# A ring of SBUF places in another order, P tiles as slices of one tile, and 21 instead of 19 weights asked for ahead, in a kernel that streams its weights

## The chip, the cores and the metric

The kernel runs on one core of one Trainium2 chip. The metric is the device time of one execution in microseconds (us). An execution is profiled once for the trace; the time is taken from several further runs.

## What is computed

Everything is float32, with 256 tokens of 1024 columns. A first block has two layers, each a token mixer with two kinds of attention and then a layer of experts; a second block has a mixer of a gated scan and a long convolution, and then a mixture of 32 experts. From the reference, cut:

```python
def first_block(x, ...):
    h = x
    for l in range(2):
        h = h + hybrid_mixer(rmsnorm(h, norm_mix[l]), w_in[l], ...)
        h = h + expert_choice_ffn(rmsnorm(h, norm_ffn[l]), w_router[l],
                                  w_expert_gate[l], w_expert_up[l], w_expert_down[l])
    return rmsnorm(h, norm_final)

def expert_choice_ffn(h, w_router, w_gate, w_up, w_down):   # 16 experts, 32 tokens each
    aff = softmax(h @ w_router)
    gate, idx = top_k(swapaxes(aff, 1, 2), 32)
    xe = h[bidx, idx]
    a, u = einsum('becd,edf->becf', xe, w_gate), einsum('becd,edf->becf', xe, w_up)
    ye = einsum('becf,efd->becd', silu(a) * u, w_down)
    return zeros_like(h).at[bidx, idx].add(gate[..., None] * ye)
...
# second block: adaLN (shift, scale and gate from silu(c) @ ada_w), a token mixer,
# then hier_moe: 4 groups of 8 experts, the best group and its best 2 experts per token
        hid = silu(einsum('td,edf->tef', t, w_gate[gi])) * einsum('td,edf->tef', t, w_up[gi]) \
            * combine[:, gi, :, None]
        out = out + einsum('tef,efd->td', hid, w_down[gi])
```

## The kernel before

The weights are some 746 MB and are read once. Nearly each is cut into pieces of 128 partitions x 2048 float32, 1 MB, and each piece is fetched by one DMA (`fetch`, issued at L58) into a tile `w`. All fetches go through SP's queue in the order of the program, each held behind the one before it (`issue_after`): a fetch whose place isn't free holds up all that are behind it.

The places are named by tags. `W` has 9 places of 1 MB and holds weights alone. `T` has 12 of the same size, which weights share with the large activations (the names in `WHOLE`: `x`, `hTa`, `qa`, `hn` and others). Small tags hold tiles of 2 KB per partition: `P` and `PT` four each (`NP`), `wh` and `wl` three each. Within a tag the places go round: the n-th tile of a tag with k places takes the place of the (n-k)-th and waits until that one's last reader is done. `K.use(places)` sets a string of tags that `chunk` goes through, one letter for each weight: for "WT" every other weight asks for a W place and every other for a T place.

The program in order of time (us of the trace): the first mixer; expert stage of layer 0 (`experts`), whose later part is interleaved with the mixer of layer 1 (`ahead`); expert stage of layer 1, interleaved with the preparation of the second block's filters and context states (`prep`); the token mixer (`token_mixer`); routing, and the MoE (`moe`, `moe_round`, `moe_quad`) to the end. Ahead of each expert stage a prefetch asks for the first weights while the mixer and the routing still work: `ROOM`, 19 tags, in the two layers, and `ROOM2`, 16 tags, in the MoE. Behind it the ring is "WT" (layer 0), `FEW` (layer 1) or "WWTWT" (MoE). In the layers a weight of `w_eg` is used by 4 instructions in L810, which the trace shows as 8 rows, two for each float32 matmul, and gives its place back after them; a MoE weight of `w2eg` is used likewise in L1485, where two weights are used in turns, a quarter of their 16 rows each. Gather matmuls (L889, L1458) lie in between while the gathered tokens of a group of experts are built. The last matmuls of the stages are L863 (`w_ed`) and L1524 (`w2ed`).

In the mixers a weight of a projection is split on the way: ScalarE rounds 512 of its columns to `wh` (L101), VectorE or POOL takes the remainder to `wl` (L102), and each product is three matmuls (L121 to L123), hTa with wh, hTb with wh, hTa with wl. A weight is thus 48 matmuls.

Attention works in rounds on tiles of tag P: mask and maximum (VectorE, L414), exponential (ScalarE, L417), scaling (VectorE, L506), transposes (PE, L434). Tag P also holds `gb` (`ada_gate`, L632 and below: a 256 KB row of biases that is fetched behind the four `ada` weights of a gate), `gs` (the gate and up products of an expert) and `yt` (a product of the MoE). `ada_gate` runs twice: in the token mixer, ahead of its weights (w2z, w2q, ...), where L174 (the squares of a norm, `sq`) was the last to use the place that `gb` takes; and behind the routing, ahead of the prefetch of the MoE, where POOL's `h` of L1317 was the last to read it.

At the start of the token mixer eight tiles `ht` (L1050, ScalarE, tag PT) are cast to `hTa` (L1051) and their remainder to `hTb` (L1052), both on VectorE.

Of the kernel before, what the change touches and what calls it, by code (L numbers as in the profile page):

```python
# [2 lines left out]

# [1 line left out]

# [4 lines left out]
F = mybir.dt.float32  # L10
# [7 lines left out]
T, D = 256, 1024  # L18
# [4 lines left out]
PW = 2048  # L23
# [9 lines left out]
class Core:  # L33
    def __init__(self, ctx, tc, A):
        self.tc, self.nc, self.A = tc, tc.nc, A
        self.const = ctx.enter_context(tc.tile_pool(name="const", bufs=1))
        self.sb = ctx.enter_context(tc.tile_pool(name="sb", bufs=1))
        self.ps = ctx.enter_context(tc.tile_pool(name="ps", bufs=1, space=PSUM))
        self.flip = self.nsplit = self.nchunk = 0

        self.share = 4
        self.after = nullcontext
        self.idle, self.pre, self.sent = (), [], None
        self.use("W")

    def load(self, name, shape, dt=F):
        t = self.const.tile(shape, dt, name=name)
        self.fetch(t, name)
        return t

    def use(self, places):

        self.ring = cycle(places)

    def fetch(self, out, src):

# [3 lines left out]
    def chunk(self, src, parts=1):  # L60

        tag = next(self.ring)
        t = self.sb.tile([128, PW], F, name="w", tag=tag, bufs=PLACES[tag])
        n = src.shape[1] // parts
        for i in range(parts):
            self.fetch(t[:, i * n:(i + 1) * n], src[:, i * n:(i + 1) * n])
        return t

    def next_chunk(self, src, parts=1):
        return self.pre.pop(0) if self.pre else self.chunk(src, parts)  # L70
# [3 lines left out]

    def t(self, shape, name, bufs=1, tag=None, dt=F):
        tag = tag or name
        if tag in WHOLE:
            tag, bufs = "T", PLACES["T"]
        return self.sb.tile(shape, dt, name=name, tag=tag, bufs=bufs)
# [122 lines left out]
class Quarters:  # L202

    shape = (128, PW)
# [9 lines left out]
class Ahead:  # L214
# [14 lines left out]
    def dest(self, j):  # L229

        for t, n, o in ((self.qk[0], 4, 0), (self.qk[1], 2, 0), (self.raw, 4, 0), (self.qk[1], 1, 4), (self.Ga, 4, 0), (self.Gb, 4, 0)):
            if j < n:
                return t[:, o + 2 * j:o + 2 * j + 2, :]
            j -= n
# [57 lines left out]
HEAD = ((1, 3), (0, 3))  # L292

WHOLE = {"x", "hTa", "hTb", "qa", "qb", "qc", "V", "G", "hgw", "hn", "ob"}
ROOM2 = "TWWTTTTWWTTTWWWW"
ROOM, FEW = "TWWWWTTTTTTWWTTTWWW", "WWWWTWWWWWT"
PLACES = {"W": 9, "T": 12}
NP = 4
SMALL = {"P": NP, "PT": NP, "wh": 3, "wl": 3, "oa": 2}
BANKS = {"mm": 2, "sc": 2, "tp": 2, "acc": 2}  # L300
# [21 lines left out]

def mixer(K, h, l, ada, first=None, ahead=None):
    nc, A = K.nc, K.A
    if ahead:
        x = ahead.x
        ahead.turned(3)
    else:
        w_in = iter(A["w_in"])

        K.idle = range(K.nsplit + HEAD[l][0], K.nsplit + HEAD[l][1])
        x = K.pair("hT")
        K.transposed(h, lambda kb, p: K.split_to(x[0][:, kb, :], x[1][:, kb, :], p, K.gmix[:, l, kb:kb + 1]),
                     banks=("tp", "sc"))
# [286 lines left out]
def ada_gate(K, g):  # L621

    nc = K.nc
    p = K.bank("acc")
    for c in range(4):
        w = K.chunk(K.A["ada"][2, 4 * g + c])
        with K.after():
            for j in range(4):
                nc.tensor.matmul(p[32 * j:32 * j + 32, :], lhsT=K.cs32[:, 2 * c + j // 2, :],
                                 rhs=w[:, j * 512:(j + 1) * 512], start=(c == 0), stop=(c == 3),  # L630
                                 tile_position=(0, 32 * j))
    gb = K.t([128, 512], "gb", NP, tag="P")  # L632
    K.fetch(gb, K.A["gtb"][g])
    K.ms = K.t([128, 512], "ms", tag="wr")
    nc.vector.tensor_add(K.ms, p, gb)
# [81 lines left out]
def experts(K, h, l, mix, ada, prep, ahead=None):  # L717
    nc, A = K.nc, K.A
# [3 lines left out]
    next(rt)  # L722
    for _ in mix:
        next(rt)
    q = K.logits
    rs = K.rstd(h, dve=False, tag="oa")
    lg = K.t([128, 2, NE], "lg")
# [64 lines left out]

    K.use(ROOM)
    ws = [K.chunk(A["w_eg"][l, i // KD, i % KD]) for i in range(len(ROOM))]
    K.use("WT" if ahead else FEW)
    hid, Ge = [], []
    gw = K.t([128, 4], "gw4")
    for e in range(NE):
        if e == 2:
            for _ in gather(1):  # L800
                pass
        oh, xT = ohs[e // 8], xTs[e // 8]
        gu = K.bank("mm")
        for k in range(KD):
            if e >= 4 and k % 3 == 2:
                next(prep, None)
            next(ga, None)
            w = ws.pop(0) if ws else K.chunk(A["w_eg"][l, e, k])
            for j in range(4):
                nc.tensor.matmul(gu[32 * j:32 * j + 32, :], lhsT=xT[:, k, (e % 8) * CAP:(e % 8 + 1) * CAP],  # L810
                                 rhs=w[:, j * 512:(j + 1) * 512], start=(k == 0), stop=(k == KD - 1),
                                 tile_position=(0, 32 * j))
        if e == 0:
            for _ in ada:
                pass
        if e % 8 == 0:
            hid.append(K.t([128, 8, 4, 64], "hid", tag=own[e // 8]))
        gs = K.t([128, 512], "gs", NP, tag="P")
        K.copy(gs, gu)
        p = K.bank("tp")  # L820
        for fb in range(4):
            nc.tensor.transpose(p[:, fb * 128:(fb + 1) * 128], gs[:, fb * 128:(fb + 1) * 128], K.ident)  # L822
        pv = p.rearrange("p (a b) -> p a b", a=4)
        sg = K.t([128, 512], "sg", NP, tag="PT")[:, :256].rearrange("p (a b) -> p a b", a=4)
        nc.scalar.activation(sg, pv[:, :, 0:64], AF.Silu)  # L825
        nc.vector.tensor_mul(hid[-1][:, e % 8], pv[:, :, 64:128], sg)  # L826
        if e % 8 == 7:

            p, q = K.bank("tp"), K.bank("acc")
            for y in range(2):  # L830
                for tt in range(2):
                    o4 = oh[:, tt, 4 * y:4 * y + 4].rearrange("p a b -> p (a b)")
                    nc.tensor.transpose(p[:, (2 * y + tt) * 128:(2 * y + tt + 1) * 128], o4, K.ident)
                for tt in range(2):
                    o4 = oh[:, tt, 4 * y:4 * y + 4].rearrange("p a b -> p (a b)")
                    nc.tensor.matmul(q[:, 4 * y:4 * y + 4], lhsT=o4, rhs=aff[:, tt, e - 7 + 4 * y:e - 3 + 4 * y],
                                     start=(tt == 0), stop=(tt == 1))
                for x in range(4):
                    nc.vector.tensor_copy(gw[32 * x:32 * x + 32, e // 8 * 2 + y:e // 8 * 2 + y + 1],
                                          q[32 * x:32 * x + 32, 4 * y + x:4 * y + x + 1])  # L840
            Ge.append(K.t([128, 2, T], "Ge4", 2, tag="oa", dt=FR))
            K.copy(Ge[-1].rearrange("p a b -> p (a b)"), p)
# [188 lines left out]

def token_mixer(K, h):
    nc, A, tc = K.nc, K.A, K.tc

    sc = K.t([128, 2, D], "sincos", tag="V")
    K.fetch(sc, "sincos")
# [9 lines left out]
    x = K.pair("hT")  # L1046
# [282 lines left out]
def moe(K, h, mix):  # L1329
    nc, A, tc = K.nc, K.A, K.tc  # L1330
# [11 lines left out]
    next(rt)  # L1342
    for _ in mix:
        next(rt)
    q = K.logits
    rs = K.rstd(h, dve=False, tag="oa")
    K.after = lambda: tc.issue_after(K.routed.ins)
# [79 lines left out]

    K.use(ROOM2)
    K.pre = [K.chunk(A["w2eg"][2 * i + x, c]) for i in range(2) for c in range(4) for x in range(2)]
    K.use("WWTWT")  # L1430

    def gate(*args):
        spread_gate(*args)
# [36 lines left out]
def moe_quad(K, h, xT, oh, cmb, e, i, gate):  # L1470

    nc, A = K.nc, K.A
    hid = []
    work = K.t([128, 2, 1024], "work", tag="G")
    for pr in range(2):
        gu = K.bank("mm")
        for c in range(4):
            ws = [K.next_chunk(A["w2eg"][e + 2 * pr + x, c]) for x in range(2)]
            for kk in range(2):
                k = 2 * c + kk  # L1480
                for x in range(2):
                    for j in range(2):
                        o = 64 * x + 32 * j
                        y = (i + 2 * pr + x) * CAP2
# [3 lines left out]
        gs = work[:, pr, 0:512]  # L1488
# [27 lines left out]
    for hf in range(2):  # L1516
        sl = slice(hf * 512, (hf + 1) * 512)
        dn = K.bank("acc")
        end = e + 4 + hf == NE2 + 1

        wd = [K.next_chunk(A["w2ed"][e + x, hf], 4 if end and x == 3 else 1) for x in range(4)]
        for c in range(4):
            for x in range(4):
                nc.tensor.matmul(dn[32 * x:32 * x + 32, :], lhsT=hid[x][:, c, :], rhs=wd[x][:, c * 512:(c + 1) * 512],  # L1524
                                 start=(c == 0), stop=(c == 3), tile_position=(0, 32 * x))
        y = K.t([128, 512], "yt", NP, tag="P")
        nc.vector.scalar_tensor_tensor(y, dn, gw, K.gt[:, 1, sl], op0=OP.mult, op1=OP.mult)
        hi, lo = yd[:, 0, sl], yd[:, 1, sl]
        K.split_to(hi, lo, y)
        for tt in range(2):  # L1530
            p = K.bank("sc")
            for n, part_ in enumerate((hi, lo)):
                nc.tensor.matmul(p, lhsT=Ge[:, tt * 128:(tt + 1) * 128], rhs=part_, start=(n == 0), stop=(n == 1))
            hs = h[:, tt, sl]
            nc.vector.tensor_add(hs, p, hs)
# [214 lines left out]
```

## Time and profile before

| | |
|---|---|
| median of 3 runs | 2229.97 us (2227.25 to 2230.5) |
| the profiled execution, its own time | 2231.4 us |
| its span in the trace | 2229.6 us |
| PE busy | 1803.5 us, 81% |
| DVE, ACT, POOL busy | 761.1, 600.3, 222.2 us |
| read from HBM | 745.74 MB, 335 GB/s over the span |
| mean granted TensorE clock | 0.915 |

Times of the trace count from the span's start. PE, ACT, DVE, POOL and SP are TensorE, ScalarE, VectorE, GpSimd and SyncE. The busy share of PE is a mean over stages: in the expert stages the DMA engines run at up to 422 GB/s and PE waits, in the mixers PE is full and the DMA engines are not. SP only issues DMAs; its waits are those of the queue of weights.

### The profile page before, as it was taken

How to read it: one execution, taken by the hardware profiler on the slowest of the kernel's cores; microseconds unless marked ns; L12 is line 12 of the kernel's file. 1: busy time of each engine (PE TensorE's matmuls, PEld its weight loads, DVE VectorE, ACT ScalarE, POOL GpSimd, SP SyncE). 2: the span in 40 equal slices, each digit the busy share in tenths (PEclk: the TensorE clock that was granted, in tenths of full speed). 3: DMA queues.
4: the chain of work that ended last, by engine and by line, in shares of the span. 5: the costliest groups of instructions: out<-in, count | busy, mean ns of one | idle time of the engine just before them, and what ended most of it. 6: DMA issues, size and time to landing. Idle time of an engine off the chain costs nothing.

```text
span 2229.6 us, 30070 instructions
## 1 busy us (share of the span) xinstructions
PE 1803.5 (81%) x12172; PEld 1017.9 (46%) x12172; DVE 761.1 (34%) x1696; ACT 600.3 (27%) x1191; POOL 222.2 (10%) x183
## 2 busy tenths in 40 slices
PE   8999996666699998987788666789999867676765
PEld 8888631110277776841234123368888412121211
DVE  5666510000045588532111111157557311111112
ACT  4666410000033357620125100055245200000000
POOL 2111200000011122300000000033134000000000
PEclk9999997777799999997799778889999999999998
DMA  8445779999999953569999999984223999999996
GB/s 342 149 146 207 313 311 420 422 421 421 421 418 419 414 210 151 216 264 399 420 420 420 421 419 420 418 337 156 76 70 149 418 420 421 420 421 421 421 421 284
DMA packets 108442, 748.83 MB, mean 336 GB/s; under 512 B 14120, under 2 KB 14537, under 8 KB 18697
## 3 DMA queue, kind: packets, MB, share of 16 engines
q1 hardware_dynamic: 107752, 745.79, 82.3%
q8 instruction: 98, 1.61, 0.3%
q10 hardware_dynamic: 544, 1.05, 0.1%
q14 instruction: 48, 0.39, 0.1%
HBM read 745.74 MB, written 1.05 MB: 335 GB/s over the span
## 4 chain that ended last, share of the span: by engine, by line
PE 40%; DMA 29%; issue 22%; DVE 6%; ACT 2%; POOL 0%; POOLq 0%; SPq 0%; ACTq 0%; DVEq 0%
DMA w<-in_w_eg 18%; DMA w<-in_w_ed 9%; PE mm L121 7%; PE mm L122 6%; PE mm L123 6%; PE acc L863 4%; PE mm L810 3%; PE sc L889 2%; DVE wl L102 1%; PE acc L518 1%; DMA w<-in_w2z 1%; PE acc L949 1%; PE acc L1228 1%; DMA cx<-in_ctx 1%; PE sc L122 1%
## 5 line engine op out<-in xcount | busy, mean ns | idle before, releaser
L810 PE MATMUL mm<-w,xT 128*32 128x512 f32 x2048 | 327.8, 743 | 116.6 <-DMA w<-in_w_eg 116.2
L101 ACT ACTIVATE wh<-w 128x512 fp32r<-128x512 f32 x384 | 239.9, 630 | 290.5 <-PE mm L122 218.0
L121 PE MATMUL mm<-hTa,wh 128*128 128x256 f32 x960 | 281.0, 294 | 5.6 <-DVE Ga L245 1.7
L123 PE MATMUL mm<-hTa,wl 128*128 128x256 f32 x960 | 274.2, 288 | 1.9 <-DVE wl L102 1.6
L122 PE MATMUL mm<-hTb,wh 128*128 128x256 f32 x960 | 272.5, 285 | 2.2 <-DVE hTb L113 1.6
L102 DVE TENSOR_TENSOR wl<-w,wh 128x512 fp32r<-128x512 f32 x286 | 220.1, 775 | 108.9 <-ACT wh L101 106.1
L1485 PE MATMUL mm<-w,xT 128*32 128x512 f32 x1024 | 176.9, 613 | 71.9 <-DMA w<-in_w2eg 71.4
L863 PE MATMUL acc<-w,hid 128*32 128x256 f32 x2048 | 184.7, 449 | 62.3 <-DMA w<-in_w_ed 62.3
L102 POOL TENSOR_TENSOR wl<-w,wh 128x512 fp32r<-128x512 f32 x98 | 129.0, 1317 | 901.9 <-ACT wh L101 803.9
L810 PEld LDWEIGHTS mm<-w,xT 128*32 128x32 f32 x2048 | 51.3, 120 | 329.6 <-DMA w<-in_w_eg 271.6
L121 PEld LDWEIGHTS mm<-hTa,wh 128*128 128x128 f32 x960 | 181.8, 190 | 28.4 <-issue 15.7
L123 PEld LDWEIGHTS mm<-hTa,wl 128*128 128x128 f32 x960 | 181.0, 190 | 10.6 <-issue 3.4
L122 PEld LDWEIGHTS mm<-hTb,wh 128*128 128x128 f32 x960 | 182.0, 190 | 6.2 <-issue 2.4
L863 PEld LDWEIGHTS acc<-w,hid 128*32 128x32 f32 x2048 | 80.5, 128 | 148.6 <-DMA w<-in_w_ed 83.1
L1524 PE MATMUL acc<-w,work 128*32 128x512 f32 x512 | 94.9, 640 | 32.9 <-DMA w<-in_w2ed 32.9
L1485 PEld LDWEIGHTS mm<-w,xT 128*32 128x32 f32 x1024 | 34.2, 110 | 189.1 <-DMA w<-in_w2eg 140.8
L178 POOL TENSOR_TENSOR rs<-rs,mhalf 128x2 f32<-128x2 f32 x9 | 6.8, 751 | 1008.4 <-DVE rs L177 1008.4
L826 DVE TENSOR_TENSOR hid<-tp,sg 128x256 f32<-128x256 f32 x32 | 13.6, 425 | 216.8 <-ACT sg L825 216.8
L113 DVE SCALAR_TENSOR_TENSOR yd<-acc,gw,yd 128x256 fp32r<-128x256 f32 x32 | 15.5, 483 | 181.2 <-ACT yd L112 181.2
L112 ACT ACTIVATE yd<-acc,gw 128x256 fp32r<-128x256 f32 x32 | 15.2, 475 | 220.0 <-PE acc L863 220.0
L91 DVE COPY gs<-mm 128x512 f32<-128x512 f32 x16 | 11.1, 692 | 181.5 <-PE mm L810 181.5
L825 ACT ACTIVATE sg<-tp 128x256 f32<-128x256 f32 x32 | 12.3, 384 | 218.3 <-PE tp L822 218.3
(468 smaller groups left out, 2471.8 us busy)
## 6 DMA issues: line engine op xcount, KB each, us to landing
w<-in_w_eg SPq DMA_DIRECT2D x256, 1024.0 KB, 19.8
w<-in_w_ed SPq DMA_DIRECT2D x128, 1024.0 KB, 18.5
w<-in_w2eg SPq DMA_DIRECT2D x128, 1024.0 KB, 19.8
w<-in_w2ed SPq DMA_DIRECT2D x63, 1024.0 KB, 19.8
w<-in_ada SPq DMA_DIRECT2D x24, 1024.0 KB, 11.7
w<-in_w_in SPq DMA_DIRECT2D x22, 1024.0 KB, 7.2
w<-in_wk SPq DMA_DIRECT2D x20, 1024.0 KB, 17.7
w<-in_w_b SPq DMA_DIRECT2D x8, 1024.0 KB, 6.0
```

The costliest lines, as they stand in the source:

```text
L101: self.hi = nc.scalar.activation(hi, src, AF.Copy)
L102: (nc.gpsimd if n in self.idle or n % self.share == self.share - 1 else nc.vector).tensor_tensor(lo, src, hi.bitcast(F), OP.subtract)
L121: mm(out, lhsT=l[0], rhs=r[0], start=start, stop=False)
L122: mm(out, lhsT=l[0], rhs=r[1], start=False, stop=False)
L123: mm(out, lhsT=l[1], rhs=r[0], start=False, stop=stop)
L518: nc.tensor.matmul(po[half * 64:half * 64 + 64, :T], lhsT=V[:, kt, c:c + 64], rhs=PTs[half][:, kt * 256:(kt + 1) * 256], start=(kt == 0), ...
L810: nc.tensor.matmul(gu[32 * j:32 * j + 32, :], lhsT=xT[:, k, (e % 8) * CAP:(e % 8 + 1) * CAP], rhs=w[:, j * 512:(j + 1) * 512], start=(k == ...
L863: nc.tensor.matmul(dn[32 * x:32 * x + 32, :T], lhsT=hid[e // 8][:, e % 8, f, hh * 32:hh * 32 + 32], rhs=ws[x][:, fb * T:(fb + 1) * T], sta ...
L889: nc.tensor.matmul(p[:, :T], lhsT=hn[:, tt, kb * 128:(kb + 1) * 128], rhs=oh[:, tt].rearrange("p a b -> p (a b)"), start=(tt == 0), stop=( ...
L949: nc.tensor.matmul(p[:, :T], lhsT=w[:, o:o + 128], rhs=cT[:, k, :], start=(k == 0), stop=(k == KD - 1))
L1485: nc.tensor.matmul(gu[o:o + 32, :], lhsT=xT[:, k, y:y + CAP2], rhs=ws[x][:, (2 * kk + j) * 512:(2 * kk + j + 1) * 512], start=(k == 0), st ...
L1524: nc.tensor.matmul(dn[32 * x:32 * x + 32, :], lhsT=hid[x][:, c, :], rhs=wd[x][:, c * 512:(c + 1) * 512], start=(c == 0), stop=(c == 3), ti ...
```

## The change

The prefetches become longer: 21 weights in the layers and 18 in the MoE (16 of `w2eg` and the first two of `w2ed`). One of them, the letter "Q", lies in four quarters of 256 KB in three `wh` places and one `wl` place; one more lies in a 13th T place. Behind the prefetch the ring repeats the tags of the prefetch in its own order (`AGAIN`, `AGAIN2`), without the first two T (which become activations) and without Q; in layer 1 `AGAIN` runs once and then `FEW`. The 13th T place comes from tag P: a P tile is now one of four slices of 512 columns of one T tile (`K.held`), which is taken anew where `K.held` is set to None. `gb`, `gs` and `yt` move from tag P to tag PT.

```diff
-    def use(self, places):
-        self.ring = cycle(places)
+    def use(self, places, first=""):
+        self.ring = chain(first, cycle(places))
...
     def chunk(self, src, parts=1):
         tag = next(self.ring)
+        if tag == "Q":
+            return self.quarters(src, ("wh", "wh", "wh", "wl"))
...
+    def quarters(self, src, tags):
+        ts = []
+        for i, tag in enumerate(tags):
+            ts.append(self.sb.tile([128, 512], F, name="w4", tag=tag, bufs=SMALL[tag]))
+            self.fetch(ts[-1], src[:, i * 512:(i + 1) * 512])
+        return Quarters(ts)
...
         tag = tag or name
+        if tag == "P":
+            if self.held is None:
+                self.held = self.sb.tile([128, PW], F, name="P4", tag="T", bufs=PLACES["T"]), cycle(range(0, PW, 512))
+            o = next(self.held[1])
+            return self.held[0][:, o:o + shape[1]]
...
-ROOM2 = "TWWTTTTWWTTTWWWW"
-ROOM, FEW = "TWWWWTTTTTTWWTTTWWW", "WWWWTWWWWWT"
-PLACES = {"W": 9, "T": 12}
+AGAIN, AGAIN2 = "WWWWTTTTTTWWTTTWWW", "WWTTTTWWTTTWWWW"
+ROOM2 = "TTWWTTTTWWTTQTWWWW"
+ROOM, FEW = "TTWWWWTTTTTTWWTTQTWWW", "WWWWTWWWWWT"
+PLACES = {"W": 9, "T": 13}
...
-    gb = K.t([128, 512], "gb", NP, tag="P")
+    gb = K.t([128, 512], "gb", NP, tag="PT")
...
-    K.use("WT" if ahead else FEW)
+    K.use(AGAIN if ahead else FEW, AGAIN)
...
-        gs = K.t([128, 512], "gs", NP, tag="P")
+        gs = K.t([128, 512], "gs", NP, tag="PT")
...
+    K.pre += [K.chunk(A["w2ed"][x, 0]) for x in range(len(ROOM2) - 16)]
-    K.use("WWTWT")
+    K.use(AGAIN2)
...
-        y = K.t([128, 512], "yt", NP, tag="P")
+        y = K.t([128, 512], "yt", NP, tag="PT")
```

`K.held = None` is added at the start of `mixer` and `token_mixer` and in both routings. Line numbers behind the first changes are some 16 to 23 higher in the changed kernel; L58 stays.

Two places in the order of the instructions. On SP, the `gb` of the token mixer and the weights behind it; the brackets give the engines whose signals an instruction waits for (DMAHW is the queue itself). Before:

```order
509 L58 DMA w<-in_ada 128x2048 [waits DMAHW6_49,PE_49]
510 L58 DMA gb<-in_gtb 128x512 [waits DMAHW7_49,Activation_49]
511 L58 DMA w<-in_w2z 128x2048 [waits DMAHW0_49,PE_49]
512 L58 DMA w<-in_w2z 128x2048 [waits DMAHW1_49,PE_49]
515 L58 DMA w<-in_w2q 128x2048 [waits DMAHW4_49,PE_49]
```

and of the change:

```order
515 L58 DMA w<-in_ada 128x2048 [waits DMAHW4_49,PE_49]
516 L58 DMA gb<-in_gtb 128x512 [waits DMAHW5_49,DVE_49,Activation_49]
517 L58 DMA w<-in_w2z 128x2048 [waits DMAHW6_49,PE_49]
518 L58 DMA w<-in_w2z 128x2048 [waits DMAHW7_49,PE_49]
521 L58 DMA w<-in_w2q 128x2048 [waits DMAHW2_49,PE_49]
```

`gb` stands where it stood, and now waits for VectorE too, for the subtraction that is the last to read the fifth `ht`. On VectorE, in the same place of the program, the casts and subtractions of the eight `ht`, `ms` (which adds `gb`) and the first `wl` of w2z. Before:

```order
955 L635 TENSOR_TENSOR ms<-acc,gb 128x512
956 L1051 CAST hTa<-ht 128x256
957 L1052 TENSOR_TENSOR hTb<-ht,hTa 128x256
958 L1051 CAST hTa<-ht 128x256
959 L102 TENSOR_TENSOR wl<-w,wh 128x512
960 L1052 TENSOR_TENSOR hTb<-ht,hTa 128x256
961 L102 TENSOR_TENSOR wl<-w,wh 128x512
```

and of the change:

```order
966 L1073 TENSOR_TENSOR hTb<-ht,hTa 128x256 x2
967 L1072 CAST hTa<-ht 128x256
968 L1073 TENSOR_TENSOR hTb<-ht,hTa 128x256
969 L1072 CAST hTa<-ht 128x256
970 L1073 TENSOR_TENSOR hTb<-ht,hTa 128x256 x2
971 L654 TENSOR_TENSOR ms<-acc,gb 128x512
972 L118 TENSOR_TENSOR wl<-w,wh 128x512 x15
```

`ms` and all of `wl` have moved behind the eight subtractions. And on SP, the second `gb`, behind the routing, with the prefetch of the MoE behind it. Before:

```order
550 L58 DMA w<-in_ada 128x2048 [waits DMAHW7_49,DVE_49,Pool_49]
551 L58 DMA gb<-in_gtb 128x512 [waits DMAHW0_49,Activation_49,Pool_49]
552 L58 DMA w<-in_w2eg 128x2048 [waits DMAHW1_49,PE_49]
553 L58 DMA w<-in_w2eg 128x2048 [waits DMAHW2_49]
554 L58 DMA w<-in_w2eg 128x2048 [waits DMAHW3_49]
```

and of the change:

```order
556 L58 DMA w<-in_ada 128x2048 [waits DMAHW5_49,DVE_49,Pool_49]
557 L58 DMA gb<-in_gtb 128x512 [waits DMAHW6_49]
558 L58 DMA w<-in_w2eg 128x2048 [waits DMAHW7_49,PE_49]
559 L58 DMA w<-in_w2eg 128x2048 [waits DMAHW0_49,PE_49]
560 L58 DMA w<-in_w2eg 128x2048 [waits DMAHW1_49,DVE_49,Pool_49]
```

This `gb` waits for no engine any more; the weights behind it wait each for the readers of its own place.

## Rows read from the trace of the kernel before

**Rows 1.** The page: busy tenths in 40 equal slices of the span.

```profile
PE   8999996666699998987788666789999867676765
DMA  8445779999999953569999999984223999999996
```

**Rows 2.** The page: the chain that ended last, its shares by line.

```profile
DMA w<-in_w_eg 18%; DMA w<-in_w_ed 9%; PE mm L121 7%; PE mm L122 6%; PE mm L123 6%; PE acc L863 4%; PE mm L810 3%; PE sc L889 2%; DVE wl L102 1%; PE acc L518 1%; DMA w<-in_w2z 1%; PE acc L949 1%; PE acc L1228 1%; DMA cx<-in_ctx 1%; PE sc L122 1%
```

**Rows 3.** Waits of SP's queue: us in total, times, the longest.

```profile
SPq L58 <- PE mm L810: 118.3, 48, 12.8
...
SPq L58 <- POOL h L1317: 18.8, 1, 18.8
...
SPq L58 <- ACT sq L174: 10.2, 1, 10.2
```

**Rows 4.** Stretches: length, busy us of each engine, PEclk, DMA share, GB/s.

```profile
360.00:620.00 260.00, 168.19 (x1030) 36.70 (x1034) 14.40 (x27) 11.25 (x24) 0.00 (x0) 0.75 1.01 421
620.00:770.00 150.00, 150.00 (x1419) 116.06 (x1412) 78.97 (x126) 51.93 (x92) 20.34 (x17) 1.00 1.01 417
...
1225.00:1446.00 221.00, 150.25 (x1290) 59.63 (x1290) 25.84 (x54) 16.01 (x30) 0.00 (x0) 0.81 1.01 420
1463.60:1468.00 4.40, 2.56 (x14) 1.81 (x11) 2.24 (x5) 2.73 (x4) 0.98 (x2) 0.50 0.97 389
...
1550.00:1650.00 100.00, 100.00 (x713) 81.95 (x712) 52.15 (x115) 28.81 (x50) 23.43 (x19) 1.00 0.24 85
...
1850.00:2205.00 355.00, 244.87 (x1368) 70.73 (x1369) 50.84 (x103) 23.04 (x44) 0.00 (x0) 0.97 1.01 421
```

**Rows 5.** The same view, around the three prefetches.

```profile
277.80:301.60 23.80, 23.80 (x142) 11.80 (x140) 6.41 (x24) 3.93 (x7) 0.00 (x0) 0.96 0.39 147
...
967.80:1010.00 42.20, 40.59 (x270) 16.95 (x270) 5.32 (x11) 6.93 (x13) 0.00 (x0) 0.98 0.60 230
...
1701.30:1726.10 24.80, 21.89 (x121) 18.12 (x120) 21.33 (x39) 11.30 (x23) 12.99 (x11) 1.00 0.00 1
1726.10:1771.00 44.90, 38.74 (x216) 21.07 (x215) 20.63 (x67) 15.08 (x29) 4.92 (x4) 0.92 0.99 407
```

**Rows 6.** The chain in order of time, layers 0 and 1: start, us, what.

```profile
285.01 0.99 PE mm L810 x8
...
287.07 1.00 PE mm L810 x8
...
973.93 0.99 PE mm L810 x8
```

**Rows 7.** Line 58 (the fetches) between 283 and 303 us.

```profile
DMA to landing us min/median/max: 4.7/11.4/15.2
```

**Rows 8.** Timeline of PE at the MoE's start: start, us, line, operation, count.

```profile
1745.93 3.64 PE L629 MATMUL acc<-w,cs 128*32 128x512 f32 x32
...
1765.51 3.63 PE L1485 MATMUL mm<-w,xT 128*32 128x512 f32 x28
```

**Rows 9.** Timeline of the token mixer's start: all engines, and PE alone.

```profile
1460.78 0.33 SPq L58 DMA_DIRECT2D gb<-in_gtb  x1
...
1467.76 1.15 ACT L101 ACTIVATE wh<-w 128x512 fp32r<-128x512 f32 x2 [0.15 <-DMA w<-in_w2z]
...
1468.44 0.58 PE L121 MATMUL mm<-hTa,wh 128*128 128x256 f32 x1
...
1470.48 2.49 ACT L1050 ACTIVATE ht<-tp,mod,A 128x256 f32<-128x256 f32 x4
...
1476.81 0.28 PE L123 MATMUL mm<-hTa,wl 128*128 128x256 f32 x1
```

**Rows 10.** Instructions on P tiles: count, ns shortest, median and longest.

```profile
L417 ACT ACTIVATE P<-P,m x80: 492/506/725, 78.4 to 890.6; 128x256 f32<-128x256 f32 x64, 128x512 f32<-128x512 f32 x16
...
L414 DVE CUSTOM_DVE_ANT_0 P<-sc,negd,nsink x64: 361/483/486, 125.5 to 888.7; 128x256 f32<-128x256 f32 x64
L506 DVE TENSOR_SCALAR P<-P,r x64: 341/349/1368, 134.4 to 894.3; 128x256 f32<-128x256 f32 x64
```

More of the change, by code (lines that the diff above doesn't have):

```diff
@@ L1 @@
 from contextlib import ExitStack, nullcontext
-from itertools import cycle, islice
+from itertools import chain, cycle, islice
 import numpy as np
@@ L42, in __init__ @@
         self.after = nullcontext
-        self.idle, self.pre, self.sent = (), [], None
+        self.idle, self.pre, self.sent, self.held = (), [], None, None
         self.use("W")
@@ L324, in mixer @@
     nc, A = K.nc, K.A
+    K.held = None
     if ahead:
@@ L724, in experts @@
         next(rt)
+    K.held = None
     q = K.logits
@@ L1033, in token_mixer @@
     nc, A, tc = K.nc, K.A, K.tc
+    K.held = None
     sc = K.t([128, 2, D], "sincos", tag="V")
@@ L1344, in moe @@
         next(rt)
+    K.held = None
     q = K.logits
```

## The prediction

> **What bounds the kernel now.** I read the page first. Its slices show two kinds of stretch: long ones in which the DMA engines are full and PE is not, and shorter ones with PE full and the DMA engines half empty [rows 1]. The chain that ended last gives 27% of the span to the transfers of the expert weights w_eg and w_ed alone [rows 2]; the reader is to see that bringing a weight earlier pays only where the DMA engines stand still just ahead of a stretch that they bound. One 1 MB weight (1.049 million bytes) at 421 GB/s takes 2.49 us [rows 4], so whatever lets the stream of weights run without a break from an earlier moment is worth 2.49 us for each weight that it is ahead.
>
> Then the DMA queue's own waits [rows 3]. Most are the ring of places doing its work. Three are not: SP waits 118.3 us in 48 pieces for the first matmuls of the experts (the longest 12.8 us), 18.8 us in one piece for POOL's h of L1317, and 10.2 us in one piece for ScalarE's sq of L174. The two single ones are the two fetches of `gb`. Windows around the three prefetches [rows 5] then show what these waits cost.
>
> **Layer 0, the first weights.** Between 277.80 and 301.60 us the DMA engines moved 147 GB/s for 23.8 us, which is 3.34 weights [rows 5]; behind it they are full [rows 1, 4]. The prefetch of 19 had landed when that window opens, so 22.3 weights had been moved at 301.60. The places are the reason: the third weight is done with at 286.00 (285.01 + 0.99), the fourth at 288.07, one every 2.06 us [rows 6], but "WT" asks for a T place second, and the first T in line is that of the seventh weight, so SP stands for up to 12.8 us [rows 3] with free W places behind it. After the change the 20th and 21st weight lie in places that nobody has to give back. They cost 2 x 2.49 us more of DMA, at worst until 282.8, and so land before the 22nd is asked for, at 286.00, when the third weight's place comes back. From issue to landing takes 4.7 us on an idle queue [rows 7], so the 22nd lands at 290.7, with its bytes some 0.6 us earlier (an estimate); places then come back every 2.06 us, faster than the stream needs them. At 301.60 the stream has 22 + 11.5/2.49 = 26.6 weights instead of 22.3: 4.3 x 2.49 = **10.7 us earlier**. Until 620 us the stretch follows the DMA engines (360 to 620: DMA share 1.01, PE busy for 168 of 260 us [rows 4]). From 620 to 770 PE is busy for all 150 us [rows 4], but the DMA share there is 1.01 as well; PE enters it 10.7 us earlier and leaves it so.
>
> **Layer 1** is the same with a larger gap, since "WWWWTWWWWWT" asks for the places still less in the order in which they return. From 967.80 to 1010.00 the engines moved 230 GB/s, 9.3 weights, 28.3 with the prefetch [rows 5]. After: 21 weights by 972.8 at the latest, the third place back at 974.92 (973.93 + 0.99) [rows 6], the 22nd weight there at 979.7. By 1010.00 the stream holds 22 + 30.9/2.49 = 34.4, 6.1 more: **15.2 us**. One place that comes back late may take 1 to 2 of them again (an estimate); I take **14.5**. Up to 1446 the DMA share stays at 1.01 [rows 4].
>
> **The MoE.** All its weights stand behind `gb` on SP's one queue, and `gb` waits for the slot of tag P that POOL reads last in L1317 [rows 3]; from 1701.30 to 1726.10 the DMA engines carry 1 GB/s [rows 5]. In PT the slot is free, as the order of the change shows: `gb` waits for no engine there, so this wait goes. It can't all be gained: of the 18 places that the prefetch now asks for, the mixer and the routing hold the last until the four `ada` weights are done with, whose matmuls end at 1749.57. And further places come back only with the experts' matmuls: the third pair of weights (16 matmuls, the last 12 of them the first of the 28 in the row from 1765.51, 0.13 us apart) gives the first of its two places back at the eighth of these, 1766.6 [rows 8]. So 20 weights are in by about 1768 (an estimate), and the 21st, asked for at 1766.6, lands at 1771.3, without a break from there. Before, 407 GB/s for 44.9 us moved 17.4 weights by 1771.00, 0.7 of them `gb` and `gf` (256 and 512 KB): 16.7 [rows 5]. The lead is 4.2 weights by bytes, 10.5 us; landings on a full queue come later behind their bytes than on an idle one, so up to 12.5 (an estimate). I take **11.5 us**. Nearly all that follows, 1850 to 2205, has the DMA share at 1.01 and PE busy for 245 of 355 us [rows 4], so the lead reaches the end.
>
> **What the change costs.** The other `gb`, in the token mixer, now takes the slot of the fifth `ht`. Before, it was issued at 1460.78, and the eight `ht` were written by ScalarE until 1472.97, the last four in the row from 1470.48, so the fifth at 1471.1. ScalarE had made three wh ahead of it (two in 1.15 us [rows 9]), which now have no weight to work on yet; without them the fifth is there at about 1469.6, and its subtraction on VectorE done at 1470.5 (both estimates). Behind `gb` on SP stand all weights of the token mixer, w2z first. Before, its first matmul ran at 1468.44, 7.7 us after the issue of `gb`; so now at 1470.5 + 7.7 = 1478.2. The 48 matmuls of one weight start 0.12 us apart (0.28 is the duration of a pipelined one) and take 5.7 us where nothing holds them; before they had to wait for hTa and hTb piece by piece and ended at 1477.09 [rows 9]. After, everything but the weight is ready, so it ends at 1478.2 + 5.7 = 1483.9, and with a slower clock at the start about 1485. **Loss 7 to 9, I take 8 us.** Next in line are PE-bound stretches (100 of 100 us busy from 1550 [rows 4]), which carry it. Its lower end is 3 us, if the next weights, which then arrive together, let PE skip a wait that it has today.
> The clock: it is at 0.50, 1.2 GHz, from 1463.6 to 1468.0, where PE was busy for 2.56 of 4.4 us [rows 4]. All 48 matmuls at that level cost 5.7 us more: the upper end, 13.7 us.
> The Trainium skill, "TensorE: Matmul & The Clock Gate", HAM oscillation, says that a wait for data between pieces of work throttles the array again and that the next piece starts cold; the 0.50 above agrees. By it the loss lies nearer to 13.7, as in rival (c).
>
> **Parts at nothing.** The P tiles are still four slots of 2 KB, now slices of one T tile; the order of each engine shows the same instructions but for the moves told above, and almost none of those on P waits for another engine than before. `gs` and `yt` in PT: they and `sg` take their slots once per expert, that is per eight weights, 8 x 2.49 = 20 us apart. Nine more DMAs (a weight in four quarters, three times) are issued while SP has slack. In layer 0 there is room for slow quarters until 286.00.
>
> **Sum.** -10.7 - 14.5 - 11.5 + 8 = -28.7. The profiled execution took 2231.4 us (span 2229.6), the median is 2229.97; from the median, **2201 us**.
>
> **Rivals.**
> (a) The token mixer loses next to nothing, since its PE work later takes up the slack: 2193. Against it: PE has no slack from 1550 to 1650.
> (b) One lead is not carried: layer 0's is lost in the PE-full stretch 620 to 770, or layer 1's in a chain of waits that does not start from a weight. For it: both engines are full there at once. One lead less: 2212 to 2215.
> (c) The clock stays at 1.2 GHz for the whole first w2z weight, since PE stands still longer ahead of it than today: the loss is 13.7 instead of 8, 2207. For it: the 0.50 ahead of w2z today; against it: today's first weight had a mean clock well above that, its matmuls getting 0.12 us apart within it.
> (d) The order of the places is worth nothing, because the return order differs from the one written out; only two weights more per prefetch count, 3 x 5.0 = 15, less 8: 2223. Against it: the seventh weight's place is asked for second, and the rows have the gap.
> (e) Slower: the four slices of one tile are held as one thing, so that each round on P (mask and maximum 0.48, exponential 0.51, scaling 0.35 [rows 10], and transposes) waits for the round before to be read. A mixer has 40 rounds. With some 0.6 us of transposes a round is 1.9 us long (an estimate), of which VectorE's 0.83 are paid in any case. So at most 40 x 1.1 = 44 us a mixer, 88 in two, 2289; it outweighs the gain from 0.36 us per round. Against it: the slices are addressed apart, and the waits in the order have not grown.
>
> **How the numbers follow.** The forecast (2194 to 2208 with its terms' bounds) 0.50; (a) 0.13; (b) 0.15; (c) 0.08; (d) 0.07; (e) 0.04; 0.03 for losses that about cancel the gain. Range: from (a) with the byte-against-landing bounds to the far end of (b), 2187 to 2215; it leaves out (d), (e) and the rest, 0.14, and some of the edges. A measurement here can tell 0.2%, 4.5 us, from no change: faster 0.93, same 0.03, slower 0.04.
>
> **What would show it.** Right: DMA share 1.0 from about 288 and from about 978 on; no stretch at 0.00 before the MoE's first weights; SP's wait for L1317 gone and one of some 10 us for VectorE's subtraction before w2z in its place; the wait for the experts' first matmuls down to many short pieces. Wrong: DMA pauses of several us after the prefetch; a new wait in the mixers for a P slice; PE idle above 1 us between 620 and 770; w2z's first matmul within 3 us of where it was.

## The result, and the profile after

The changed kernel takes 2204.55 us (median of 4 runs, 2203.01 to 2205.20) against 2229.28 before: a ratio of 0.9889, 95% interval 0.9872 to 0.9906, 24.7 us less. Its profiled execution took 2205.11 us, with a span of 2203.3, 26.3 below that of before.

The page first: the slices of PE and of the DMA engines, which stand against [rows 1].

```profile
PE   8999996666699998988788666679999877676765
DMA  8445889999999954589999999974217999999996
```

The low digits of DMA ahead of the three full stretches have risen (5 7 7 to 5 8 8 in layer 0, 3 5 6 to 4 5 8 in layer 1, 2 3 to 1 7 at the MoE); the full stretches are all but as they were. SP's waits, as in [rows 3] (us in total, times, the longest):

```profile
SPq L58 <- PE mm L830: 84.9, 40, 14.8
...
SPq L58 <- DVE hTb L1073: 20.4, 1, 20.4
```

The wait for POOL's h ahead of the MoE is gone, and the wait for sq has become one for the subtraction hTb, 20.4 us long instead of 10.2. The wait for the experts' first matmuls is shorter in total, but not in short pieces as I had said: with a longer prefetch SP reaches the first place that is not free sooner. In layer 1 it stands there for 14.8 us, until 963.5. Only the first part of that wait costs nothing, while the transfers asked for before it are still running; then the DMA engines run dry. The two parts, and the same pause in layer 0:

```profile
948.70:958.00 9.30, 5.87 (x20) 5.02 (x20) 6.33 (x18) 0.24 (x1) 0.00 (x0) 0.63 1.00 417
958.00:963.50 5.50, 5.47 (x35) 1.93 (x33) 0.97 (x2) 0.71 (x2) 0.00 (x0) 1.00 0.02 6
...
277.80:285.30 7.50, 7.50 (x50) 4.29 (x49) 3.44 (x18) 0.95 (x2) 0.00 (x0) 0.95 0.01 2
```

So 5.5 us without transfers are left in layer 1 and 7.5 us in layer 0, and at the MoE some 7 us behind its first weight (1686 to 1693, 20 GB/s). Whether still more weights asked for ahead would fill them was not tried.

The stretches of [rows 4, 5], the later ones moved by what the kernel was ahead there:

```profile
277.80:301.60 23.80, 23.80 (x149) 11.35 (x147) 6.40 (x24) 4.39 (x8) 0.00 (x0) 0.98 0.65 249
...
610.00:760.00 150.00, 150.00 (x1404) 115.92 (x1393) 80.68 (x126) 52.08 (x92) 20.73 (x18) 1.00 1.01 418
956.50:998.70 42.20, 41.42 (x269) 17.19 (x272) 5.32 (x11) 7.01 (x14) 0.00 (x0) 0.98 0.84 340
...
1530.00:1630.00 100.00, 100.00 (x716) 82.06 (x715) 52.45 (x116) 28.59 (x50) 24.32 (x18) 1.00 0.24 85
1682.90:1707.70 24.80, 21.95 (x121) 18.16 (x120) 21.33 (x39) 11.30 (x23) 13.00 (x11) 1.00 0.69 282
1707.70:1752.60 44.90, 38.41 (x210) 20.84 (x209) 20.84 (x67) 13.15 (x27) 4.93 (x4) 0.89 0.87 335
```

The last column is the one to read: 147 GB/s became 249, 230 became 340, 1 became 282. The last stretch fell from 407 to 335, but over it and the one ahead of it the engines moved 22.0 MB instead of 18.3. PE does about the same work in each stretch as before; what grew is what the DMA engines carried beside it.

Where the time came from can be read from the same instruction in both traces, at the joints of the stages. Of before, from the chain in order of time and from PE's timeline (VectorE's placing of the tokens at the start of layer 1's experts; the first matmul of the token mixer's gate; the transposes of the MoE's routing):

```profile
961.60 1.22 DVE place L764
```
```profile
1454.55 1.07 PE L629 MATMUL acc<-w,cs 128*32 128x512 f32 x8 [0.75 <-DMA w<-in_ada]
...
1739.89 2.02 PE L193 MATMUL tp<-ident,h 128*128 128x128 f32 x8 [1.65 <-POOL h L1317]
```

and of after, the same views:

```profile
950.16 1.22 DVE place L784
```
```profile
1430.48 1.06 PE L648 MATMUL acc<-w,cs 128*32 128x512 f32 x8 [1.09 <-DMA w<-in_ada]
...
1721.48 1.79 PE L209 MATMUL tp<-ident,h 128*128 128x128 f32 x8 [1.66 <-POOL h L1338]
```

| stage | ahead at its end | won in it | predicted |
|---|---|---|---|
| layer 0 and the mixer behind it | 11.4 us | 11.4 | 10.7 |
| layer 1 | 24.1 | 12.6 | 14.5 |
| token mixer | 18.4 | -5.7 | -8 |
| MoE, to the end of the span | 26.3 | 7.9 | 11.5 |

The first line counts from the span's start. "Ahead" is the start in the trace of before less the start in the trace of after.

### The profile page after: what moved, and what is told of

Same layout as the page of the kernel before. It is cut to its first block, busy times and chain, and to the rows that moved or that the text cites. A ratio compares the mean times of both kernels' runs of the same rounds, so it can differ in the third digit from the quotient of the medians.

```text
span 2203.3 us, 30089 instructions
## 1 busy us (share of the span) xinstructions
PE 1796.9 (82%) x12172; PEld 1015.9 (46%) x12172; DVE 762.0 (35%) x1696; ACT 599.5 (27%) x1191; POOL 221.3 (10%) x183
## 4 chain that ended last, share of the span: by engine, by line
PE 40%; DMA 30%; issue 22%; DVE 6%; ACT 1%; POOL 0%; POOLq 0%; DVEq 0%; SPq 0%; ACTq 0%
DMA w<-in_w_eg 21%; DMA w<-in_w_ed 9%; PE mm L137 7%; PE mm L139 7%; PE mm L138 7%; PE acc L883 4%; PE mm L830 2%; PE sc L909 2%; DVE wl L118 1%; DMA w<-in_w2z 1%; PE acc L537 1%; PE acc L1249 1%; PE sc L138 1%; PE sc L139 1%; PE tp L453 1%
## 5 line engine op out<-in xcount | busy, mean ns | idle before, releaser
L1547 PEld LDWEIGHTS acc<-w,work 128*32 128x32 f32 x512 | 21.5, 119 | 100.0 <-issue 52.7
```

## The experiments

A ratio is that to the kernel before, run on the same chip in the same rounds. A single execution can be 3 us off ahead of the first expert stage already, so stages are compared within a trace.

**The token mixer's gb out of the way of w2z.** In the changed kernel, one line:

```diff
-    gb = K.t([128, 512], "gb", NP, tag="PT")
+    gb = K.t([128, 512], "gb", NP, tag="PT" if g else "P")
```

> The changed kernel, but the bias row gb of the token mixer alone goes back to tag P (a slice of the held tile); the one of the MoE stays in PT. Theory A (SP's queue stands behind the fifth ht, and the token mixer's first weight comes later by what the trace after shows, 5.6 us net): w2z is asked for some 10 us earlier and the time falls by 5 to 6 us against the changed kernel, to about 2199 us, ratio to before 0.9865. Rival B (the pause is taken up by slack later): within 2 us of the changed kernel, 2203 to 2206.

Measured: 2195.54 us (2194.49 to 2196.07), ratio 0.9844, interval 0.9831 to 0.9858: 9 us below the changed kernel, more than theory A's 5 to 6, and rival B is out. This version beats both kernels. SP's timeline, with gb as a P tile, and PE's first matmul of w2z and its transposes of the MoE's routing:

```profile
1435.75 0.33 SPq L58 DMA_DIRECT2D P<-in_gtb  x1
1436.17 2.03 SPq L58 DMA_DIRECT2D w<-in_w2z  x4
```
```profile
1443.27 0.56 PE L137 MATMUL mm<-hTa,wh 128*128 128x256 f32 x1
...
1715.54 2.09 PE L209 MATMUL tp<-ident,h 128*128 128x128 f32 x8 [1.66 <-POOL h L1338]
```

7.5 us lie between gb and the first matmul, as before (7.7). This matmul is 25.2 us ahead of before, and the transposes are 24.4 us ahead, so the rest of this stage loses 0.8 us, where the changed kernel lost 5.7 from the gate to the transposes. The other 3 us were won in the MoE: the span is 2193.8 us, so from the transposes to its end 11.5 us are won instead of 7.9. The reason follows under "The MoE's start".

**The same move alone, in the kernel before.**

```diff
-    gb = K.t([128, 512], "gb", NP, tag="P")
+    gb = K.t([128, 512], "gb", NP, tag="P" if g else "PT")
```

> The kernel before, with the token mixer's gb alone moved to PT. Theory A: SP's wait for sq becomes a wait of about 20 us for the fifth subtraction, w2z lands 7 to 8 us later, of which PE's later work gives back about 2: slower by 5 to 7 us, 2235 us, ratio 1.0025. Rival B (the pause is hidden): no change. By the first sum (8 us): 2238.

Measured: 2237.19 us, ratio 1.0028 (1.0017 to 1.0038), 6.7 us slower than the 2230.48 of before in the same rounds: theory A. The wait is the one expected:

```profile
SPq L58 <- DVE hTb L1052: 21.3, 1, 21.3
```

**The MoE's gb alone, in the kernel before** (the tag is PT where g is 1, else P).

> The kernel before, with the MoE's gb alone moved to PT: 16 weights ahead, the old string behind them. Theory A (the pause of 25 us without a transfer goes, and what then sets the lead is when the experts' matmuls give places back, not the number asked for): about 10 us faster, 2219 to 2221, as much as the whole change gains in the MoE. Rival B (the two further weights and the order are part of the MoE's gain): 5 us faster or less.

Measured: 2223.36 us, ratio 0.9973 (0.9961 to 0.9985), 7.1 us less, with a span 8.7 shorter. Theory A was a little high, but this one tag gives nearly all that the change wins in the MoE (7.9). The stretches that answer to the last two of [rows 5]:

```profile
1700.70:1725.50 24.80, 21.89 (x121) 18.13 (x121) 21.32 (x39) 11.38 (x22) 12.98 (x11) 1.00 0.84 331
1725.50:1770.40 44.90, 38.35 (x221) 20.04 (x219) 21.04 (x69) 15.31 (x30) 5.00 (x5) 0.96 0.80 308
```

Over both, 331 x 24.8 + 308 x 44.9 is 22.0 MB; the changed kernel carried 282 x 24.8 + 335 x 44.9, which is 22.0 MB, too. Two weights more ahead and another string did not bring more by this point, which fits theory A: the places that come back set it. Further on, rival B is not out. From the routing's transposes to the end of the span this run wins 8.2 us, and the runs below that have 18 weights, the new string and no delay of the experts win 11.0 to 11.5. The two weights and the string may thus be worth some 3 us, hidden in the changed kernel by the delay that follows; no run has them alone.

**The MoE's start.** Why the changed kernel won no more there: PE's timeline of before and then of after, the first matmul on the mask rt, the first experts' matmuls, and the row in which the third pair's place comes back.

```profile
1752.33 0.41 PE L1394 MATMUL tp<-rt,cb 128*128 128x64 f32 x2 [2.76 <-issue]
...
1756.83 1.44 PE L1485 MATMUL mm<-w,xT 128*32 128x512 f32 x8
```
```profile
1734.94 0.41 PE L1416 MATMUL tp<-rt,cb 128*128 128x64 f32 x2 [3.78 <-issue]
...
1739.60 1.94 PE L1508 MATMUL mm<-w,xT 128*32 128x512 f32 x8
...
1749.37 3.63 PE L1508 MATMUL mm<-w,xT 128*32 128x512 f32 x28
```

The changed kernel is 18.4 us ahead at the transposes, 17.4 at rt, 17.2 at the first expert, 16.1 at the row of 28. The first of it is an order on VectorE that the change also moved, and that I had not looked at. Of before, and of after:

```profile
1752.01 0.21 DVE L1390 TENSOR_TENSOR rt<-cb 128x64 f32<-128x64 f32 x1
1752.15 0.17 DVE L1408 TENSOR_TENSOR cb<-cb 128x16 f32<-128x16 f32 x1
```
```profile
1733.90 0.18 DVE L1434 TENSOR_TENSOR cb<-cb 128x16 f32<-128x16 f32 x1
1734.01 0.69 DVE L654 TENSOR_TENSOR ms<-acc,gb 128x512 f32<-128x512 f32 x1
1734.62 0.21 DVE L1412 TENSOR_TENSOR rt<-cb 128x64 f32<-128x64 f32 x1
```

L1434 is the last of the sums of the combine weights (L1412 of before); five of these sums, 0.2 us each, now stand ahead of rt, for which the gather waits. Most of the rest went to slower first pairs (1.94 us instead of 1.44). To undo the order:

```diff
-    nc.vector.tensor_tensor(msk...
+    placed = nc.vector.tensor_tensor(msk...
...
-    nc.vector.tensor_reduce(sm, el, axis=AX.X, op=OP.add)
+    with tc.issue_after(placed.ins):
+        nc.vector.tensor_reduce(sm, el, axis=AX.X, op=OP.add)
```

> The changed kernel, with one order more in the routing of the MoE: the sums of the combine weights on VectorE (the part of the routing that the gather does not need) may start only when the mask of the routed tokens has been issued, so that the mask rt stands ahead of them. Theory A (the MoE's lead is set by when the experts' first matmuls give their places back; they start 1.2 us late in the changed kernel since rt is written behind seven small operations of 0.2 us, and their clock is lower for the first pairs): 2 to 3 us faster than the changed kernel, 2202. Rival B (the MoE's lead is set by the transfers): no change, 2204.5.

Measured: 2202.79 us (2201.61 to 2207.60), ratio 0.9869 (0.9854 to 0.9884). The trace has what was expected:

```profile
1727.29 1.42 PE L209 MATMUL tp<-ident,h 128*128 128x128 f32 x8 [1.66 <-POOL h L1338]
...
1738.05 0.41 PE L1416 MATMUL tp<-rt,cb 128*128 128x64 f32 x2 [2.27 <-issue]
```

PE is idle for 1.5 us less ahead of rt than after the change, but the intervals overlap, so the times alone do not tell A from B. The stages do. From the transposes to the end of its span of 2205.8 us (the slowest of its four executions, by what earlier stages lost) this run wins 11.2 us against before. The run with gb in P, whose idle time ahead of rt is 2.77 us, wins 11.5. The changed kernel with its 3.78 us wins 7.9, and the two runs below that change strings alone and keep that delay (3.79 both) win 9.2 and 8.0. So with this prefetch an early rt is worth some 2 to 3.5 us in this stage, near theory A's 2 to 3. The idle time ahead of rt is 1 to 1.5 us of that. The first pairs are as slow here as in the changed kernel (1.94 us), so slow first pairs alone do not cost it; what makes the rest is not shown. With gb in P as well:

> The changed kernel with the token mixer's gb in tag P and the same order in the routing. In the run with gb in P alone VectorE's order has rt ahead of most of the sums already, so theory A gives 0.5 to 1.5 us more than that run: 2194 to 2195, ratio to before 0.984. Rival B: as that run, 2195.5.

Measured: 2195.53 us, ratio 0.9844 (0.9831 to 0.9858), the same as with gb in P alone, where the gap is 2.77 us without any help. Here it is 2.26 us, and the MoE wins 11.0. So theory A's further 0.5 to 1.5 us are not there, or too small to see.

**The old strings behind the longer prefetches.** In the changed kernel:

```diff
-    K.use(AGAIN if ahead else FEW, AGAIN)
+    K.use("WT" if ahead else FEW)
...
-    K.use(AGAIN2)
+    K.use("WWTWT")
```

> The changed kernel with 21, 21 and 18 weights asked for ahead, but with the old strings behind them (WT, FEW, WWTWT). Theory A (a place asked for out of turn holds the queue): in layer 0 the 22nd weight is still asked for when the third place comes back, but the 23rd waits for the eighth weight's place; its stream is then some 5 us ahead of before instead of 10.7, in layer 1 some 6 instead of 12 to 13; the MoE keeps its lead, since its places come back late in any order. Time about 2214 us, 8 to 12 above the changed kernel. Rival B (only the number asked for ahead counts): as the changed kernel, 2203 to 2206.

Measured: 2220.90 us, ratio 0.9954 (0.9939 to 0.9969): 16.4 us above the changed kernel (14.5 by the two ratios), more than theory A's 8 to 12; rival B is out. The stretch behind layer 0's prefetch, and the two joints around layer 1:

```profile
277.80:301.60 23.80, 23.80 (x142) 11.87 (x142) 6.09 (x24) 3.93 (x7) 0.00 (x0) 0.95 0.42 162
```
```profile
955.47 1.22 DVE place L784
```
```profile
1447.55 1.06 PE L648 MATMUL acc<-w,cs 128*32 128x512 f32 x8 [0.72 <-DMA w<-in_ada]
```

It is 6.1 us ahead of before at the first joint and 7.0 at the second. The miss is layer 1: 0.9 us won there instead of the expected 6.

**The new strings alone, in the kernel before** (`use` with `first`, AGAIN and AGAIN2; prefetches, places and tags as before).

> The kernel before, with the new strings alone behind the prefetches (AGAIN, then FEW in layer 1; AGAIN2 in the MoE): still 19, 19 and 16 weights ahead, 12 T places, both gb in P. Theory A (a place asked for out of turn holds the queue): the 20th weight of layer 0 still lands at 288, and the stream runs from there, 8 to 9 us ahead of before; in layer 1 some 9 to 10; in the MoE nothing, since all stands behind gb: 2212 to 2214 us, ratio 0.992. Rival B (only the number asked for ahead counts): no change. If order and number added up without overlap, the order would be worth what the run with the old strings lost, 16 us, too.

Measured: 2214.51 us, ratio 0.9921 (0.9897 to 0.9945), 17 us less: theory A in time. The same stretch and joints:

```profile
277.80:301.60 23.80, 23.80 (x147) 11.73 (x150) 6.40 (x24) 3.92 (x7) 0.00 (x0) 0.98 0.73 281
```
```profile
953.77 1.22 DVE place L765
```
```profile
1438.29 1.06 PE L630 MATMUL acc<-w,cs 128*32 128x512 f32 x8
```

With the weights asked for ahead, 21 + 162 x 23.8 / 1049 = 24.7 weights have been moved by 301.60 with the longer prefetch and the old string, 19 + 6.4 = 25.4 with the new string alone, 26.6 with both, against 22.3 before: 2.4, 3.1 and 4.3 weights. (Where 21 are asked for, the last lands as the window opens; so some tenths are too much; and an execution that is late by then, as that of the old strings, shows too little.) In layer 0 the number and the order are thus worth nearly the same (6.1 and 7.8 us ahead at the first joint), and both together less than their sum. In layer 1 nearly all is the order: alone it wins 8.4 us (16.3 ahead at the second joint), the number alone 0.9, both 12.6.

**The old string in layer 1 alone.**

```diff
-    K.use(AGAIN if ahead else FEW, AGAIN)
+    K.use(AGAIN if ahead else FEW, AGAIN if ahead else "")
```

> The changed kernel with the old string behind the prefetch in layer 1 alone (FEW at once, without AGAIN). Theory A (from the traces: the lead won in layer 1 is 12.6 us with the new order and 1.2 us with 21 weights and the old one): 10 to 12 us slower than the changed kernel, 2215. Rival B (by the give-back times of the trace before, two weights more are worth 5 us of the 12.6): 7 us slower, 2211. Rival C (the number alone): no change.

Measured: 2217.29 us, ratio 0.9937 (0.9920 to 0.9953), 12.7 above the changed kernel (10.7 by the two ratios). Theory A's 10 to 12 is nearest and C is out; the times leave room for B's 7. In the trace layer 1 wins 2.7 us, nearer to A's 1.2 than to B's 5. The stretch behind layer 1's prefetch, 340 GB/s in the changed kernel:

```profile
960.30:1002.50 42.20, 41.45 (x275) 16.70 (x277) 5.74 (x12) 7.32 (x14) 0.00 (x0) 0.99 0.59 224
```

As slow as before (230): with FEW at once, two weights more are followed by the same pause.

**P slices alone, in the kernel before** (T of 13 places, P tiles from a held T tile in `t`, `K.held = None` in `mixer` and `token_mixer`).

> The kernel before, with tag P alone changed into four slices of a 13th T tile (gb, gs and yt stay in P; the prefetches and the strings stay). Theory A (slices are waited for each by itself): within 4 us of before, 2227 to 2234, the rest from T places given out in another order. Rival E of the prediction (the tile is held as one): up to 88 us slower, seen in both mixers.

Measured: 2232.49 us, ratio 1.000 (0.999 to 1.001): theory A, and rival E's slowdown is out. The second mixer, PE busy 182.68 of 200 us against 180.75 before:

```profile
770.00:970.00 200.00, 182.68 (x1211) 140.99 (x1215) 152.62 (x395) 114.03 (x265) 48.36 (x38) 0.97 0.58 224
```

## Why the prediction came out

The forecast was 2201, and 2204.55 is inside the likeliest case's own range. All four terms have the forecast sign. In the layers and the token mixer the mechanism came out too, and the misses are sizes; in the MoE one step failed. That the sum came out so near is in part luck: layer 1 and the MoE won 5.5 us less than forecast, and layer 0 and the token mixer came out 3.0 us better.

*Layer 0.* 10.7 was forecast, 11.4 found, with 0.7 won in the mixer behind (its first transposes run 10.75 us earlier, at 604.60 instead of 615.35). The places came back as read: the third weight is done at 285.25, and the 22nd is asked for less than 0.1 us later.

```profile
284.26 0.99 PE mm L830 x8
```
```profile
L58 SPq DMA_DIRECT2D w<-in_w_eg x8: 327/328/328, 285.3 to 299.2; - x8
```

The lead went through the 150 us in which PE is full, 610 to 760, so rival (b) fell: PE and the stream both come that much earlier, and neither has to wait for the other.

*Layer 1.* 14.5 forecast, 12.6 found. The stretch carried 340 x 42.2, 13.7 weights instead of 9.3, which is 11 us. The two weights more of the prefetch are another 5.0 us, less the 1.5 us at the start of the stretch in which the prefetch was still landing: 14.5 at the end of the stretch, as forecast. I had allowed 1 to 2 us for a place that comes back late and subtracted 0.7. The DMA share is 0.99 from 1000 to 1020, so no late place shows there. What was lost came behind the stretch, while small fetches (the filter's weights) ran between the large ones. Of after and of before, the same 46 us of the stream:

```profile
984.00:1030.00 46.00, 39.61 (x280) 11.85 (x280) 13.97 (x27) 3.56 (x8) 0.00 (x0) 0.93 1.00 396
```
```profile
1010.00:1056.00 46.00, 34.71 (x173) 7.97 (x172) 12.38 (x24) 2.58 (x6) 0.00 (x0) 0.74 1.02 404
```

8 GB/s less over 46 us is 0.9 us of transfers. Why these fetches took longer, and where the last 1 us went, stays open.

*Token mixer.* The fifth subtraction ended at 1446.01 and SP issued gb at 1446.07, 24.1 - 14.7 = 9.4 us late against the rest, where 9.7 was forecast. The loss at the first weight was forecast as 7 to 9. PE's timeline, the clock of the transposes ahead of the pause, and that of two stretches behind it:

```profile
1452.09 0.58 PE L137 MATMUL mm<-hTa,wh 128*128 128x256 f32 x1 [7.05 <-ACT wh L117]
...
1459.72 0.28 PE L139 MATMUL mm<-hTa,wl 128*128 128x256 f32 x1
```
```profile
1442.80:1445.10 2.30, 2.23 (x8) 1.43 (x8) 1.82 (x8) 2.16 (x4) 0.00 (x0) 0.50 0.00 0
...
1452.00:1456.00 4.00, 3.91 (x17) 3.69 (x18) 1.90 (x3) 1.70 (x4) 0.16 (x1) 0.50 1.01 426
1456.00:1460.00 4.00, 4.00 (x34) 3.83 (x33) 0.69 (x1) 2.65 (x5) 1.38 (x2) 0.98 1.01 426
```

The 48th matmul of w2z ran at 1459.72, against 1476.81 before: 17.1 us ahead instead of 24.1, a loss of 7.0. Some 1.3 us of it were given back behind, because the second weight's matmuls follow without the pause of 1.4 us that they had. The clock stood at 1.2 GHz after PE had waited 7.05 us and rose to 2.4 GHz within the weight, so rival (c) was half right on the clock (17 of the 48 matmuls at the low level) and wrong on the price: some 1.5 us instead of 5.7. The Trainium skill ("TensorE: Matmul & The Clock Gate", HAM oscillation) says that a wait for data throttles the array and that the next piece starts cold. The 0.50 at the start of w2z agrees with the cold start; that this wait lowered the clock is not shown, since the transposes ahead of it had 0.50 already. That the clock stays low through the whole piece was my reading. Rival (a) is wrong: without the pause the kernel is 9 us faster.

*MoE.* 11.5 forecast, 7.9 found. The step that failed is that the experts' matmuls give places back when they did before, less the lead: they started 1.2 us later than that, by the order on VectorE, and their first pairs were slower by another 1.1. The stream's lead is that of the place asked for last, so it loses both. With the same prefetch and an early rt, three runs win 11.0 to 11.5 us in the MoE, as forecast. Another 1.2 us went near the end of the changed kernel's trace, where one row of matmuls had a lower clock in that execution. Of before, and of after:

```profile
2201.00:2206.40 5.40, 5.32 (x26) 1.23 (x26) 0.00 (x0) 0.00 (x0) 0.00 (x0) 0.68 1.01 409
```
```profile
2173.90:2180.50 6.60, 6.49 (x26) 1.34 (x26) 0.01 (x1) 0.00 (x0) 0.00 (x0) 0.56 0.99 398
```

*The rivals on order and slices.* Rival (d), that the order is worth nothing, is out by two runs: alone it gives 17 us, and without it the change keeps 8 to 10 of its 24.7 us (8.4 by the median of the changed kernel, 9.6 by that of before in the same rounds). Its price for the number alone, 2223, was near the 2220.90 measured. Rival (e) is out: the slices alone cost nothing that these runs can tell (0.1%). The sum was made with the two leads of order and number in one, so it did not show that the strings carry some two thirds of the gain, and in layer 1 nearly all.

## What to carry to other kernels

In a queue that takes its requests in a fixed order, the order in which places are asked for counts as much as their number: write it down as the order in which the readers finish. A tile moved to another ring of buffers takes over the wait of that ring; look up who holds the slot, and what stands behind the transfer in the queue. Where a lead ends in places that an engine gives back, look at that engine's own start, and at the order of the small work ahead of it.

## What the runs showed of the hardware

TensorE's granted clock was 0.50 in the transposes ahead of the token mixer's pause of 7 us, and still 0.50 in the first 4 us of matmuls behind it (17 of them); then it was 0.98. Most of the 17 started 0.21 us apart instead of 0.12, which for all 17 is some 1.5 us (an estimate). And a transfer queue hides a wait of its issuer only as long as it has transfers to run: of the 14.8 us that SP stood for one place in the changed kernel, the DMA share was 1.00 in the first 9.3 and 0.02 in the last 5.5.
